# Queries and keys of a dilated attention placed by SBUF transfers, softmax statistics of two heads exchanged by a matmul

## The chip, the cores and the metric

One core of one Trainium2 chip runs the whole program in one launch. The metric is the device time in microseconds; a figure for a kernel is the median of its runs.

## What is computed

Two blocks on a sequence of 1024 positions and 1024 channels, in f32: an S5 mixer with a conv-GLU FFN, then a dilated attention with a second FFN. The change lies in the attention. It has 16 heads of 64 channels and three dilation groups g = 0, 1, 2 (dilation 1, 4, 16), each with queries, keys and values of its own; every group is an attention over a band of 128 steps, and the groups are merged by their log-sum-exps:

```python
for g, (_, dil) in enumerate(DILATED_GROUPS):       # dil = 1, 4, 16
    s = jnp.einsum('brnqhe,brnkhe->brnhqk', qb, kb) + bias
    s = jnp.where(valid[:, None], s, NEG_BIG)
    lse = jax.nn.logsumexp(s, axis=-1)
    p = jnp.exp(s - lse[..., None])
    o = jnp.einsum('brnhqk,brnkhe->brnqhe', p, vb)
...
wts = jax.nn.softmax(jnp.stack(lses), axis=0)
o = jnp.einsum('gblh,gblhe->blhe', wts, jnp.stack(outs))
```

## The kernel before

Every large matmul keeps f32 accuracy by splitting each operand into a high part (`wh`, a cast to fp32r) and the rest (`wl`), and issuing three matmuls, `mm3` on L88, L89 and L90. A weight of 512 KB is loaded to `raw`, cast to `wh` by ScalarE (ACT, L83), and `wl` is subtracted by VectorE (DVE, L84). The order of the instructions of every engine is fixed when the program is built: a scheduler places them by its own timeline. On the chip each engine, and the DMA queue of SyncE (SP) too, runs its list in order and waits at an instruction until its inputs and its buffer are there.

The attention (L367) runs over 8 pairs of heads; a pair fills the 128 partitions, head 0 on the lower 64 rows and head 1 on the upper 64. For each pair and each g, `proj` (L407) makes Q and K in two halves of 512 columns, 24 matmuls (`qk` in the traces) to a half, then `scores` (L463) multiplies them (`s`, L488), and DVE adds the bias and takes the row maxima (L476). `proj` of the next pair's g = 0 is issued ahead of `output` (L583) of this one, and the scheduler interleaves further. `output` takes the exponentials (`exps`, L526), the softmax factors of each head (`softmax`, L539), scales the probabilities `p1` (g = 0, L556) and `p4` (g = 1 and 2, L563), transposes them on TensorE (PE, `t`, L604) and multiplies them by V (`o`, L614), and adds the two parts to `oT` (L658), which goes to DRAM as `oscr`.

A score also is two matmuls: `qs` holds the query's high part of one head on 64 rows and its low part on the other 64, and `qs` and `kl` of K hold the key's high and low part on both halves of the rows. So each 64-row half has to reach the other half of the partitions. Before, ACT copies the PSUM result to `tmp` (named `qt`, L430, L432) and casts the 64-row halves (L436, L438), and GpSimd (POOL) subtracts the low parts (L440), with different partitions in and out.

The g = 0 rows and the g = 1, 2 rows of a query lie on different partitions, so the two softmax statistics (maximum and sum) have to be exchanged: 32 small copies of 32 partitions on DVE per head and direction pair (L551, L552), followed by `factor` (L565), once for f1 and once for f4.

The pools matter: `w` has 6 tiles, that is three split weights, in the whole program after the S5 part; `raw` has 2; PSUM has two tiles for `qk` (psA) and four for `s` and `t`, which share them (psS).

## Time and profile before

| | |
|---|---|
| median of 3 runs | 3187.31 us (3179.75 to 3188.91) |
| the profiled execution | 3185.67 us |
| its span, first to last instruction | 3183.7 us, so 1.97 us lie outside |
| busy in the span: PE, DVE, ACT, POOL | 2963.2, 1809.4, 1074.7, 721.9 us |
| mean granted clock of TensorE | 0.961 of full speed |
| the attention | from about 1410 us to 2333 us |

PE is busy for 93% of the span; where it stands still, or runs at half its clock, time is lost. The attention repeats with a period of one pair, which can be cut at the start of the first `p1` scaling of each pair (1500.31, 1612.86, ... 2175.86 us). The tail from 2175.86 us on holds the output of pair 6, the last scores and the output of pair 7, which has no further `proj` beside it.

### The profile page before, as it was taken

The page shows a single profiled execution, that of the slowest core. Times are in us where ns is not written, and L with a number is a line of the kernel's source. Part 1 is how long each engine was busy: PE and PEld are TensorE (multiplying, and loading weights), DVE is VectorE, ACT ScalarE, POOL GpSimd, SP SyncE. Part 2 cuts the span into 40 slices and gives each one's busy share as a digit, 9 for nine tenths or more (in the row PEclk, how much of TensorE's full clock was granted, in tenths as well). Part 3 has the DMA queues.
Part 4 walks back from the last instruction along what each step waited for, and adds up shares of the span by engine and source line. Part 5 has one row for each costly group of instructions (what it writes and reads, how often), then busy time and mean ns, then how long its engine had stood idle before and what let it go on. Part 6 is the DMA issues. An engine that isn't in the chain of part 4 may idle for free.

```text
span 3183.7 us, 36883 instructions
## 1 busy us (share of the span) xinstructions
PE 2963.2 (93%) x14422; PEld 2457.5 (77%) x14422; DVE 1809.4 (57%) x3348; ACT 1074.7 (34%) x1868; POOL 721.9 (23%) x543
## 2 busy tenths in 40 slices
PE   4789999999999999999898998989689999999997
PEld 3668878888888879998677777767567788888886
DVE  8964774544545541115668567666757644445446
ACT  2433332222222231126455555645523322222222
POOL 7920050000000000015335434434652300000001
PEclk8889999999999999999999999999799999999998
DMA  5232421111111232321111111111243211111111
GB/s 174 58 126 62 135 71 47 47 49 51 52 48 40 81 122 88 92 86 41 57 50 57 55 62 44 57 60 44 70 150 112 66 47 53 47 53 41 53 60 53
DMA packets 98413, 219.63 MB, mean 69 GB/s; under 512 B 9664, under 2 KB 51248, under 8 KB 98240
## 3 DMA queue, kind: packets, MB, share of 16 engines
q1 hardware_dynamic: 96128, 207.85, 20.8%
q0 software_dynamic: 2112, 9.44, 0.9%
q8 instruction: 113, 1.85, 0.2%
q14 instruction: 60, 0.49, 0.0%
HBM read 191.49 MB, written 35.20 MB: 71 GB/s over the span
## 4 chain that ended last, share of the span: by engine, by line
PE 78%; DVE 11%; POOL 5%; ACT 3%; DMA 1%; issue 1%; SPq 0%; ACTq 0%; POOLq 0%; DVEq 0%
PE dn L236 15%; PE up L89 10%; PE up L88 10%; PE up L90 10%; PE qk L88 3%; PE qk L89 3%; PE qk L90 3%; PE v L88 3%; DVE p L556 3%; PE v L89 3%; PE v L90 3%; PE o L614 3%; ACT p L533 2%; PE t L604 2%; PE s L488 2%; DVE p L563 2%
## 5 line engine op out<-in xcount | busy, mean ns | idle before, releaser
L84 DVE TENSOR_TENSOR wl<-raw,wh 128x1024 fp32r<-128x1024 f32 x261 | 339.3, 1301 | 680.4 <-ACT wh L83 675.8
L83 ACT CAST wh<-raw 128x1024 fp32r<-128x1024 f32 x261 | 274.0, 1052 | 1081.2 <-PE up L89 468.6
L88 PE MATMUL up<-hT,wh 128*128 128x512 f32 x1408 | 548.7, 391 | 12.1 <-DVE u L212 12.1
L89 PE MATMUL up<-hT,wh 128*128 128x512 f32 x1408 | 548.9, 390 | 0.7 <-DVE hT L84 0.7
L90 PE MATMUL up<-hT,wl 128*128 128x512 f32 x1408 | 548.5, 390 | 0.0
L440 POOL TENSOR_TENSOR qs<-qt,qs 64x512 fp32r<-64x512 f32 x96 | 127.4, 1327 | 1174.7 <-ACT qs L436 1140.9
L88 PEld LDWEIGHTS up<-hT,wh 128*128 128x128 f32 x1408 | 265.0, 188 | 67.5 <-issue 12.9
L440 POOL TENSOR_TENSOR kl<-qt,qs 64x512 fp32r<-64x512 f32 x192 | 255.8, 1332 | 253.9 <-PE s L488 218.8
L88 PE MATMUL qk<-hT,wh 128*128 128x512 f32 x768 | 310.6, 404 | 0.0
L89 PEld LDWEIGHTS up<-hT,wh 128*128 128x128 f32 x1408 | 265.4, 188 | 56.9 <-DVE hT L84 2.1
L90 PEld LDWEIGHTS up<-hT,wl 128*128 128x128 f32 x1408 | 265.1, 188 | 54.9
L90 PE MATMUL qk<-hT,wl 128*128 128x512 f32 x768 | 306.8, 399 | 0.0
L89 PE MATMUL qk<-hT,wh 128*128 128x512 f32 x768 | 306.4, 399 | 0.0
L212 DVE SCALAR_TENSOR_TENSOR u<-up,cw,u 128x1022 f32<-128x1022 f32 (+1 forms) x176 | 224.6, 1278 | 30.4 <-ACT u L208 28.2
L246 DVE TENSOR_TENSOR acc<-acc,dn 128x1024 f32<-128x1024 f32 x144 | 175.0, 1217 | 91.8 <-PE dn L236 89.3
L236 PE MATMUL dn<-wh,ah 128*128 128x512 f32 x704 | 216.9, 389 | 0.0
L236 PE MATMUL dn<-wl,ah 128*128 128x512 f32 x704 | 216.7, 389 | 0.0
L236 PE MATMUL dn<-wh,al 128*128 128x512 f32 x704 | 216.6, 389 | 0.0
L88 PEld LDWEIGHTS qk<-hT,wh 128*128 128x128 f32 x768 | 148.8, 194 | 30.2 <-issue 2.7
L89 PEld LDWEIGHTS qk<-hT,wh 128*128 128x128 f32 x768 | 148.1, 193 | 29.1
L90 PEld LDWEIGHTS qk<-hT,wl 128*128 128x128 f32 x768 | 147.4, 192 | 29.5
L604 PE MATMUL t<-ident,p 128*128 128x128 f32 x624 | 105.3, 316 | 64.7 <-DVE p L556 64.7
(248 smaller groups left out, 5113.9 us busy)
## 6 DMA issues: line engine op xcount, KB each, us to landing
raw<-in_w_up SPq DMA_DIRECT2D x88, 512.0 KB, 3.5
raw<-in_w_out SPq DMA_DIRECT2D x48, 512.0 KB, 3.5
raw<-in_w_down SPq DMA_DIRECT2D x44, 512.0 KB, 3.5
raw<-in_w_v SPq DMA_DIRECT2D x25, 512.0 KB, 3.6
vscr<-vs SPq DMA_DIRECT2D x48, 256.0 KB, 2.3
V<-vscr SPq DMA_DIRECT2D x24, 512.0 KB, 4.1
raw<-in_w_q SPq DMA_DIRECT2D x24, 512.0 KB, 3.6
raw<-in_w_k SPq DMA_DIRECT2D x24, 512.0 KB, 3.5
```

Source lines behind the costliest of these rows:

```text
L83: nc.scalar.copy(hi, x)
L84: (eng or nc.vector).tensor_tensor(out=lo, in0=x, in1=hi.bitcast(F32), op=ALU.subtract)
L88: nc.tensor.matmul(out, lh, rh, start=first, stop=False)
L89: nc.tensor.matmul(out, lh, rl, start=False, stop=False)
L90: nc.tensor.matmul(out, ll, rh, start=False, stop=last)
L212: nc.vector.scalar_tensor_tensor(out=tf[:, d:], in0=ps[:, : T - d], scalar=cw[:, d, ft : ft + 1], in1=tf[:, d:], op0=ALU.mult, op1=ALU.add,)
L236: nc.tensor.matmul(ps[:, h * 512 : h * 512 + 512], l_, w[wi][:, h * 512 : h * 512 + 512], start=(i == 0 and l_ is ah and wi == 0), stop=(i ...
L246: nc.vector.tensor_tensor(out=accs[tt][:], in0=accs[tt][:], in1=ps[:], op=ALU.add)
L440: nc.gpsimd.tensor_tensor(out=lo, in0=tmp[r], in1=hi.bitcast(F32), op=ALU.subtract)
L556: nc.vector.tensor_scalar(out=x, in0=x, scalar1=f1[:, n : n + 1], scalar2=None, op0=ALU.mult)
L604: nc.tensor.transpose(ps[:, i * P : i * P + P], b, net.ident[:])
L614: nc.tensor.matmul(o[64 * h : 64 * h + 64, oc], v[:, 64 * h : 64 * h + 64], pt[h], start=st, stop=sp_)
```

## The change

`proj` no longer uses GpSimd. ACT writes the high part `qh` (128x512) straight from PSUM (now the key carries the factor 0.125), DVE subtracts the low part `ql` (128x512) from PSUM, and SBUF-to-SBUF DMAs on SP's queue put the 64-row halves in place: 4 for a half of Q, 8 for a half of K, so 24 to a g, 72 to a pair and 576 in all, 64 rows of 2 KB each.

`softmax` treats both heads together. `exchange` multiplies the statistics by a mask (`bd`, DVE), and one matmul with a constant matrix `eye4` moves them to the partitions where they are wanted; four small copies read them from PSUM. There is one such matmul for the statistics, one factor chain of half the instructions, and one matmul that brings the factor back for `p4`. Head 1's `p4` is scaled by ACT, head 0's by DVE.

For room, the pool `w` goes from 6 tiles to 4 (two split weights, in the whole program after the S5 part), `values_first` keeps two weights of the first values block and not three (one more load of 512 KB in the attention), `q` goes from 9 to 10 tiles and `qt` from 2 to 4.

```diff
-    ws = [net.wload(net.a["w_v"][0, i], **({"pool": pool, "tag": "x"} if i == 3 else {})) for i in range(4)]
+    ws = [net.wload(net.a["w_v"][0, i], **({"pool": pool, "tag": "x"} if i > 1 else {})) for i in range(4)]
...
-        tmp = ap.tile([P, 512], F32, "qt", "qt")
...
+        hi, lo = (ap.tile([P, 512], F32R, "qt", n) for n in ("qh", "ql"))
...
+        if isq:
+            nc.scalar.copy(h_, i)
+            nc.vector.tensor_tensor(out=l_, in0=i, in1=h_.bitcast(F32), op=ALU.subtract)
         else:
-            nc.scalar.copy(o, i)
+            nc.scalar.mul(h_, i, 0.125)
+            nc.vector.scalar_tensor_tensor(
+                out=l_, in0=i, scalar=0.125, in1=h_.bitcast(F32), op0=ALU.mult, op1=ALU.subtract
+            )
         for h in range(2):
-            r, o = slice(64 * h, 64 * h + 64), slice(64 - 64 * h, 128 - 64 * h)
-            hi = X[h][r, sl]
-            nc.scalar.copy(hi, tmp[r])
-            if not isq:
-                nc.scalar.copy(X[h][o, sl], tmp[r])
-            for lo in [X[h][o, sl]] if isq else [kl[h][r, sl], kl[h][o, sl]]:
-                nc.gpsimd.tensor_tensor(out=lo, in0=tmp[r], in1=hi.bitcast(F32), op=ALU.subtract)
+            r = slice(64 * h, 64 * h + 64)
+            for c in range(2):
+                o = slice(64 * c, 64 * c + 64)
+                if isq:
+                    nc.sync.dma_start(X[h][o, sl].bitcast(F32), (lo if c else hi)[r].bitcast(F32))
+                else:
+                    nc.sync.dma_start(X[h][o, sl].bitcast(F32), hi[r].bitcast(F32))
+                    nc.sync.dma_start(kl[h][o, sl].bitcast(F32), lo[r].bitcast(F32))
...
+    def exchange(self, st, n, a, b):
+        bd = net.asp.tile([P, 4, 32], F32, "bd", "bd")
+        nc.vector.tensor_tensor(
+            out=bd[:, :, : 8 * n], in0=st.unsqueeze(1).broadcast_to([P, 4, 8 * n]),
+            in1=net.mask4[:].unsqueeze(2).broadcast_to([P, 4, 8 * n]), op=ALU.mult,
+        )
+        ps = net.psS.tile([P, 512], F32, "s", "x")
+        nc.tensor.matmul(
+            ps[:, : 32 * n], net.eye4[:], bd[:, :, : 8 * n], start=True, stop=True
+        )
...
+        for c in range(8):
+            for h in range(2):
+                p = self.tiles4(h)[c][1]
+                if h:
+                    nc.scalar.mul(p, p, f4[:, h, c : c + 1])
+                else:
+                    nc.vector.tensor_scalar(out=p, in0=p, scalar1=f4[:, h, c : c + 1], scalar2=None, op0=ALU.mult)
...
-        net.weight_pools(6, 2)
+        net.weight_pools(4, 2)
```

The scheduler orders everything anew. Three places of its lists follow; numbers after a name are those of its tiles, and `waits` names the engines or DMA lanes whose semaphores an instruction waits for.

First place, DVE between the exponentials of a pair and its first transposes. Before, from the last scaling of head 0's `p4` (L563) on:

```order
L563 TENSOR_SCALAR p4_1262_9222<-p4_1262_9222,e_1361_9935 128x512
L84 TENSOR_TENSOR wl_1463_10536<-raw_1461_10533,wh_1462_10535 128x1024 [waits DMAHW7_49,PE_49,Activation_49]
L576 TENSOR_TENSOR t_1370_10016<-st1_1264_9224,e_1368_10010 128x8 [waits Activation_49]
L569 TENSOR_TENSOR M_1371_10022<-st4_1265_9225,x4_1366_9975 128x8
L577 TENSOR_TENSOR ex_1369_10011<-x1_1365_9974,ex_1369_10011 128x8 [waits Activation_49]
L571 TENSOR_TENSOR e_1372_10024<-st4_1265_9225,M_1371_10022 128x8 [waits DVE_49]
L572 TENSOR_TENSOR ex_1373_10025<-x4_1366_9975,M_1371_10022 128x8
L578 TENSOR_TENSOR t_1370_10016<-t_1370_10016,ex_1369_10011 128x8 [waits DVE_49]
L579 RECIPROCAL t_1370_10016<-t_1370_10016 128x8 [waits DVE_49]
L576 TENSOR_TENSOR t_1374_10030<-st4_1265_9225,e_1372_10024 128x8 [waits Activation_49]
L577 TENSOR_TENSOR ex_1373_10025<-x4_1366_9975,ex_1373_10025 128x8 [waits Activation_49]
L580 TENSOR_TENSOR e_1368_10010<-e_1368_10010,t_1370_10016 128x8 [waits DVE_49]
```

Behind these rows stands the scaling of head 1's `p1`. Now, from the end of the one factor chain on:

```order
L584 TENSOR_TENSOR g4_1383_9962<-e_1380_9951,M_1379_9950 128x16 [waits DVE_49]
L587 TENSOR_TENSOR f1_1386_9968<-e_1380_9951,M_1379_9950 128x16
L550 TENSOR_TENSOR bd_1384_9964<-g4_1383_9962,mask4_1089_7705 128x4x16 [waits DVE_49]
L596 TENSOR_SCALAR p1_1269_9241<-p1_1269_9241,f1_1386_9968 128x128 [waits DVE_49]
L596 TENSOR_SCALAR p1_1269_9241<-p1_1269_9241,f1_1386_9968 128x256 x7
L596 TENSOR_SCALAR p1_1270_9242<-p1_1270_9242,f1_1386_9968 128x128
L596 TENSOR_SCALAR p1_1270_9242<-p1_1270_9242,f1_1386_9968 128x256 x7
L84 TENSOR_TENSOR wl_1479_10498<-raw_1477_10495,wh_1478_10497 128x1024 [waits PE_49,Activation_49]
L433 TENSOR_TENSOR ql_1457_10350<-qk_1455_10324,qh_1456_10349 128x512 [waits DMAHW4_49,DMAHW2_49,DMAHW6_49,DMAHW0_49,Activation_49]
L590 COPY f4_1382_9961<-x_1385_9966 32x16 [waits PE_49]
L590 COPY f4_1382_9961<-x_1385_9966 32x16 x3
```

The `p1` of both heads is now scaled in a row (L596, 16 instructions), ahead of all `p4`, which follows behind the four copies from the second exchange.

Second place, the change from one pair to the next: the last `s` of g = 0 or g = 1 of the next pair. PE before, from the last `s` of g = 0 on:

```order
L488 MATMUL s_1433_10312<-kl_1345_9797,qs_1334_9725 128x256
L90 MATMUL qk_1468_10572<-hT_1079_7656,wl_1463_10536 128x512
L88 MATMUL qk_1468_10572<-hT_1082_7666,wh_1462_10535 128x512
L89 MATMUL qk_1468_10572<-hT_1082_7666,wh_1462_10535 128x512
L90 MATMUL qk_1468_10572<-hT_1082_7666,wl_1463_10536 128x512
L88 MATMUL qk_1468_10572<-hT_1084_7675,wh_1462_10535 128x512
L89 MATMUL qk_1468_10572<-hT_1084_7675,wh_1462_10535 128x512
L90 MATMUL qk_1468_10572<-hT_1084_7675,wl_1463_10536 128x512
L88 MATMUL qk_1468_10572<-hT_1087_7685,wh_1462_10535 128x512
L89 MATMUL qk_1468_10572<-hT_1087_7685,wh_1462_10535 128x512
L90 MATMUL qk_1468_10572<-hT_1087_7685,wl_1463_10536 128x512
L488 MATMUL s_1455_10479<-qs_1447_10405,qs_1438_10335 128x128 [waits DVE_49,Pool_49]
```

PE now, from the end of the last but one `s` tile of g = 1 on:

```order
L495 MATMUL s_1475_10481<-qs_1462_10364,qs_1451_10290 128x256
L495 MATMUL s_1475_10481<-kl_1464_10366,qs_1451_10290 128x256
L495 MATMUL s_1476_10488<-qs_1462_10364,qs_1451_10290 128x256 [waits DVE_49]
L495 MATMUL s_1476_10488<-kl_1464_10366,qs_1451_10290 128x256
L495 MATMUL s_1476_10488<-qs_1462_10364,qs_1451_10290 128x256
L495 MATMUL s_1476_10488<-kl_1464_10366,qs_1451_10290 128x256
L88 MATMUL qk_1495_10579<-hT_1029_7405,wh_1489_10571 128x512 [waits DVE_49]
L89 MATMUL qk_1495_10579<-hT_1029_7405,wh_1489_10571 128x512
```

Before, ten `qk` stand between the `s` of g = 0 and those of g = 1. Now three `qk` stand in the middle of g = 0 and none between g = 0 and the end of g = 1; the next `qk` tile waits for DVE. DVE now, at the same place:

```order
L483 ISA mg_1436_10206 128x1
L483 ISA p4_1433_10203,mg_1436_10206<-s_1476_10488,bt_1346_9748 128x256 [waits PE_49]
L483 ISA mg_1436_10206 128x1
L483 ISA p4_1433_10203,mg_1436_10206<-s_1476_10488,bt_1346_9748 128x256
L483 ISA mg_1436_10206 128x1
L433 TENSOR_TENSOR ql_1484_10529<-qk_1482_10503,qh_1483_10528 128x512 [waits DMAHW5_49,DMAHW3_49,DMAHW6_49,DMAHW1_49,Activation_49]
L433 TENSOR_TENSOR ql_1487_10562<-qk_1485_10536,qh_1486_10561 128x512 [waits DMAHW5_49,DMAHW7_49,DMAHW2_49,Activation_49]
L436 SCALAR_TENSOR_TENSOR ql_1497_10605<-qk_1495_10579,qh_1496_10604 128x512 [waits DMAHW4_49,DMAHW3_49,Activation_49]
L84 TENSOR_TENSOR wl_1521_10791<-raw_1519_10788,wh_1520_10790 128x1024 [waits PE_49,Activation_49]
L436 SCALAR_TENSOR_TENSOR ql_1500_10642<-qk_1498_10616,qh_1499_10641 128x512 [waits DMAHW7_49,DMAHW0_49,Activation_49]
```

The low part `ql` that frees the `qk` tile (L433) stands behind all maxima (L483, ISA, with the reading of its accumulator) of g = 0 and g = 1.

Third place, SP's queue at the same change of pairs. Before, from the loads of V for the next output on:

```order
L588 DMA V_1508_10894<-vscr_7476 128x1024 [waits DMAHW3_49,PE_49]
L588 DMA V_1509_10896<-vscr_7476 128x1024 [waits DMAHW4_49,DMAHW1_49,PE_49]
L665 DMA oscr_9062<-oT_1392_10125 128x1024 [waits DMAHW5_49,DVE_49]
L75 DMA raw_1602_11425<-in_w_k 128x1024 [waits DMAHW0_49,DVE_49]
L75 DMA raw_1619_11559<-in_w_q 128x1024 [waits DMAHW2_49,DVE_49]
L453 DMA bt_1487_10737<-bscr0_2300 32x2x256 [waits DVE_49]
L453 DMA bt_1487_10737<-bscr0_2300 32x2x256 x2
```

Now:

```order
L610 DMA V_1532_10872<-vscr_7476 128x1024 [waits DMAHW5_49,PE_49]
L610 DMA V_1533_10874<-vscr_7476 128x1024 [waits DMAHW6_49,DMAHW1_49,PE_49]
L683 DMA oscr_9075<-oT_1404_10079 128x1024 [waits DMAHW7_49,DVE_49]
L446 DMA qs_1462_10364<-qh_1466_10392 64x512 [waits DMAHW0_49,PE_49]
L447 DMA kl_1464_10366<-ql_1467_10393 64x512 [waits PE_49]
L446 DMA qs_1462_10364<-qh_1466_10392 64x512 [waits DMAHW2_49]
L447 DMA kl_1464_10366<-ql_1467_10393 64x512 [waits DMAHW3_49]
L446 DMA qs_1462_10364<-qh_1469_10429 64x512 [waits DMAHW4_49]
L447 DMA kl_1464_10366<-ql_1470_10430 64x512 [waits DMAHW5_49]
L446 DMA qs_1462_10364<-qh_1469_10429 64x512 [waits DMAHW6_49]
L447 DMA kl_1464_10366<-ql_1470_10430 64x512 [waits DMAHW7_49]
```

Behind the two loads of V and the store of `oT` stand eight placements of K, g = 1, head 1; most of them also wait for an earlier DMA on the same lane (DMAHW).

## Rows read from the trace of the kernel before

**Rows 1.** The page, busy us (share of the span) and instructions of each engine.

```profile
PE 2963.2 (93%) x14422; PEld 2457.5 (77%) x14422; DVE 1809.4 (57%) x3348; ACT 1074.7 (34%) x1868; POOL 721.9 (23%) x543
```

**Rows 2.** Stretches (us): each engine busy and (instructions), clock, DMA share, GB/s.

```profile
1500.31:1612.86 112.55, 103.67 (x567) 82.85 (x566) 77.33 (x248) 60.73 (x138) 47.95 (x36) 0.95 0.18 55
...
2175.86:2290.00 114.14, 88.08 (x477) 69.18 (x475) 72.45 (x228) 57.89 (x134) 56.92 (x44) 0.87 0.16 56
```

**Rows 3.** Timeline of PE around the longest gap of a period: start us, us, instruction.

```profile
1632.80 1.97 PE L604 MATMUL t<-ident,p 128*128 128x128 f32 x8 [5.50 <-DVE p L556]
...
1638.34 0.63 PE L89 MATMUL qk<-hT,wh 128*128 128x512 f32 x1
1638.77 0.63 PE L90 MATMUL qk<-hT,wl 128*128 128x512 f32 x1
...
1642.05 0.40 PE L89 MATMUL qk<-hT,wh 128*128 128x512 f32 x1
1642.28 0.40 PE L90 MATMUL qk<-hT,wl 128*128 128x512 f32 x1
```

**Rows 4.** Timeline of DVE, scaling of the probabilities.

```profile
1612.66 8.62 DVE L556 TENSOR_SCALAR p<-p,e 128x128 f32<-128x128 f32 x8
...
1623.40 6.91 DVE L563 TENSOR_SCALAR p<-p,e 128x256 f32<-128x256 f32 x8
...
1636.84 2.73 DVE L563 TENSOR_SCALAR p<-p,e 128x256 f32<-128x256 f32 x8
...
2296.97 2.13 DVE L556 TENSOR_SCALAR p<-p,e 128x128 f32<-128x128 f32 x8
```

**Rows 5.** Groups by line and form, 1400 to 2300 us: count | busy us, mean ns.

```profile
L440 POOL TENSOR_TENSOR kl<-qt,qs 64x512 fp32r<-64x512 f32 x192 | 255.8, 1332 | 253.9 <-PE s L488 218.8 <-ACT qs L436 21.6 <-issue 2.2
...
L84 DVE TENSOR_TENSOR wl<-raw,wh 128x1024 fp32r<-128x1024 f32 x46 | 58.9, 1280 | 48.4 <-ACT wh L83 48.4
...
L533 ACT ACTIVATE p<-p,nm 128x512 f32<-128x512 f32 x64 | 45.5, 711 | 0.0
...
L579 DVE RECIPROCAL t<-t 128x8 f32<-128x8 f32 x30 | 6.0, 201 | 0.8
```

**Rows 6.** Timeline of DVE behind the last output of a pair.

```profile
1673.87 1.22 DVE L658 TENSOR_TENSOR oT<-oT,o 128x1024 f32<-128x1024 f32 x1 [5.50 <-PE o L614]
1675.01 0.28 DVE L476 CUSTOM_DVE_ANT_0 p<-s,bt 128x128 f32<-128x128 f32 x1
...
1675.22 0.42 DVE L476 CUSTOM_DVE_ANT_0 p<-s,bt 128x256 f32<-128x256 f32 x1
...
1675.56 0.42 DVE L476 CUSTOM_DVE_ANT_0 p<-s,bt 128x256 f32<-128x256 f32 x1
```

**Rows 7.** What PE waited for, 1400 to 2300 us: us, times, longest us.

```profile
PE s L488 <- DVE st L476: 16.4, 14, 1.5
```

**Rows 8.** Timeline of the SP queue: start us, us of issue, transfer, count.

```profile
1673.65 0.80 SPq L588 DMA_DIRECT2D V<-vscr  x2
1675.12 0.32 SPq L665 DMA_DIRECT2D oscr<-oT  x1
...
1716.43 1.74 SPq L453 DMA_DIRECT2D bt<-bscr  x4
```

**Rows 9.** DMA issues of the whole span: count, KB each, median us to landing.

```profile
oscr<-oT SPq DMA_DIRECT2D x7, 512.0 KB, 5.7
...
bt<-bscr SPq DMA_DIRECT2D x32, 64.0 KB, 1.9
```

**Rows 10.** The 20 us in which the DMA engines moved most, columns as in rows 2.

```profile
2340.00:2360.00 20.00, 17.17 (x72) 13.56 (x71) 5.20 (x4) 3.15 (x3) 14.67 (x6) 0.97 0.76 287
```

**Rows 11.** Timeline of POOL in the last pair.

```profile
2274.84 5.27 POOL L440 TENSOR_TENSOR kl<-qt,qs 64x512 fp32r<-64x512 f32 x4
...
2300.22 11.02 POOL L563 TENSOR_SCALAR p<-p,e 128x256 f32<-128x256 f32 x8 [3.31 <-DVE e L571]
```

**Rows 12.** What PE waited for, 225 to 460 us.

```profile
PE up L88 <- DVE u L212: 6.0, 1, 6.0
```

More of the change, by code (lines that the diff above doesn't have):

```diff
@@ L373, in attention @@
         else:
-            ws = ws + [net.wload(net.a["w_v"][0, 3], pool=ap, tag="q")]
+            ws = ws + [net.wload(net.a["w_v"][0, i], pool=ap, tag="q") for i in (2, 3)]
         for j in range(8) if blk else range(4, 8):
@@ L463, in scores @@
     def scores(self, g):
-        net, nc, ap, sp, bt = self.net, self.net.nc, self.ap, self.net.small, self.bt
+        net, nc, ap, sp, bt = self.net, self.net.nc, self.ap, self.net.asp, self.bt
         if g == 0:
@@ new lines, in softmax @@
+    def softmax(self):
+        nc, sp = self.net.nc, self.net.asp
+        t = lambda shape, n: sp.tile([P] + shape, F32, n, n)
+        st1, st4 = self.st1, self.st4
+        x = t([2, 2, 8], "x1")
+        ps = self.exchange(st4[:].rearrange("p h s c -> p (h s c)"), 4, "r", "n")
+        for r in range(4):
+            R = slice(32 * r, 32 * r + 32)
+            nc.vector.tensor_copy(
+                x[R].rearrange("p h s (n a) -> p (h s) a n", a=4), ps[R, :, :, r, :]
+            )
+        M, e, y = t([2, 8], "M"), t([2, 2, 8], "e"), t([2, 2, 8], "y")
+        nc.vector.tensor_tensor(out=M[:], in0=st1[:, :, 0], in1=x[:, :, 0], op=ALU.max)
+        for i, s in enumerate((st1, x)):
+            nc.vector.tensor_tensor(out=e[:, i], in0=s[:, :, 0], in1=M[:], op=ALU.subtract)
+        nc.scalar.activation(e[:], e[:], AF.Exp)
+        for i, s in enumerate((st1, x)):
+            nc.vector.tensor_tensor(out=y[:, i], in0=s[:, :, 1], in1=e[:, i], op=ALU.mult)
+        nc.vector.tensor_tensor(out=M[:], in0=y[:, 0], in1=y[:, 1], op=ALU.add)
+        nc.vector.reciprocal(M[:], M[:])
+        f4 = t([2, 8], "f4")
+        g = t([2, 8], "g4")
+        nc.vector.tensor_tensor(out=g[:], in0=e[:, 1], in1=M[:], op=ALU.mult)
+        ps = self.exchange(g[:].rearrange("p h c -> p (h c)"), 2, "n", "a")
+        f1 = t([2, 8], "f1")
+        nc.vector.tensor_tensor(out=f1[:], in0=e[:, 0], in1=M[:], op=ALU.mult)
+        for a in range(4):
+            A = slice(32 * a, 32 * a + 32)
+            nc.vector.tensor_copy(
+                f4[A].rearrange("p h (r n) -> p h r n", r=4), ps[A, :, :, :, a]
+            )
+        for h in range(2):
+            for n in range(8):
+                p = self.p1[h][:, n, 128 if n == 0 else 0 :]
+                nc.vector.tensor_scalar(out=p, in0=p, scalar1=f1[:, h, n : n + 1], scalar2=None, op0=ALU.mult)
+        for c in range(8):
+            for h in range(2):
+                p = self.tiles4(h)[c][1]
[3 more added lines that the diff above has]
+                    nc.vector.tensor_scalar(out=p, in0=p, scalar1=f4[:, h, c : c + 1], scalar2=None, op0=ALU.mult)
@@ L589, in output @@
             V.append(v)
-        for h in range(2):
-            if self.hp < 7:
+        if self.hp < 7:
+            for h in range(2):
                 self.exps(h)
-            f4 = self.softmax(h)
-            if self.hp == 7 and h == 0:
-                self.scale4(h, f4, nc.gpsimd)
-        if self.hp == 7:
-            self.scale4(1, f4, nc.vector)
+        self.softmax()
         def transposed(blocks):
@@ L673, in setup @@
     net.psO = net.pool("psO", ctx, PSUM, o=1)
-    return net.pool("ap", ctx, q=9, qt=2, V=2, oT=1, p1=2, p4=2, bt=1, pt=4)
+    net.asp = net.pool("asp", ctx, eye4=1, mask4=1, bd=1, x1=1, y=1, g4=1, other=2)
+    net.eye4 = net.asp.tile([P, P], F32, "eye4")
+    net.mask4 = net.asp.tile([P, 4], F32, "mask4")
+    net.nc.sync.dma_start(net.eye4[:], net.a["eye4"])
+    net.nc.sync.dma_start(net.mask4[:], net.a["mask4"])
+    return net.pool("ap", ctx, q=10, qt=4, V=2, oT=1, p1=2, p4=2, bt=1, pt=4)
 MAGIC = 12582912.0
@@ L1416, in layout @@
     o["eye16"] = np.tile(np.eye(16, dtype=np.float32), (8, 1))
+    o["eye4"] = np.tile(np.eye(32, dtype=np.float32), (4, 4))
+    o["mask4"] = np.repeat(np.eye(4, dtype=np.float32), 32, axis=0)
     o["onehot"] = bias_onehot()
```

61 lines of the change are left out of this document (11 added, 50 removed).

## The prediction

> **What bounds the kernel now.** First the page: PE is busy for 93% of the span, DVE for 57%, POOL for 23% [rows 1]. Less work on DVE, ACT or POOL is thus worth nothing by itself; time can come only out of PE's gaps, or out of stretches in which PE runs at half its clock. Then the stretches by pair: a period is 112.6 us, with 103.4 busy on PE, so 9.2 us idle, and a granted clock of 0.95 [rows 2]. Six such periods lie between 1500.31 and 2175.86 us, 112.59 on average. The longest gap is in the timeline of PE: 5.50 us until DVE has scaled `p1` of head 1, and when PE comes back, its matmuls run at the lower of the two clock levels: two neighbouring `qk` start 0.43 us apart, some microseconds later 0.23 [rows 3]. 16 `t` (8 in 1.97 us, taken as twice their full-clock time) and 9 `qk` (0.20 each) pay about 4 us; I use 4.2. A pair therefore is 103.4 - 4.2 = 99.2 us of work at full clock, 4.2 of low clock and 9.2 of idling.
>
> Why `p1` of head 1 is late stands in the order of DVE and in its timeline. Its scaling comes behind head 0's `p1` scaling (8.62 us), head 0's `p4` scaling (6.91) and the chain of factors. The same eight instructions took 2.13 us at 2297 us, and `p4` took 2.73, when POOL ran no L440 beside them [rows 4]. POOL makes four such subtractions of 1.33 us for each half of K [rows 5].
>
> **The change, part by part.** The sum is made against the profiled execution, 3185.67 us, which stands 1.6 us below the median of the runs. About 0.3% of the median, 9.6 us, is what a measurement of this kernel can tell from no change.
>
> *Gaps before the transposes.* Both heads' `p1` are now scaled one behind the other, ahead of `p4`. By the rows without POOL this is 2 x 2.13 = 4.3 us. Behind the last `s` of the pair PE has 64 `qk` ahead of the first exchange, 14.6 us at 0.23; head 1's eight exponentials, two `qh` and a weight cast on ACT are under 12 x 0.75 = 9, an exponential of 512 columns being 0.71 [rows 5]: some 5 us to spare. Between the exchanges lie 37 `qk`, 8.4 us; four copies, the chain and `bd`, 16 small instructions of 0.2 [rows 5], and one `ql` are 3.9, 4.5 to spare. Then come the scalings, 4.3, of which the first two suffice for the first `t`. The 5.50 us gap, its smaller neighbours (about 1.5 us) and the 4.2 us of low clock go. What is late next is the `pt` copy on DVE behind head 0's `p4` scaling: 2.73 + four small copies against some 4 us of `qk` and `t`; I put 1.0 us there. The two exchange matmuls cost 0.4 at most, two `t` at the low clock being 0.5 [rows 3]. ACT's new scaling of head 1's `p4`, eight passes of at most 0.71 us [rows 5], is hidden by the `o` of g = 0.
>
> *Projections.* ACT goes from five passes per half of K, and three of Q, to one each; it was hidden and stays so. DVE gains 12 `ql` a pair: a pass over 512 columns of PSUM is bounded by two passes of 256 with the bias added, 0.35 us each, thus 0.7 [rows 6], and from below by 0.35; I take 0.7. POOL's 36 L440 a pair go. Where `ql` waits for nobody it is hidden; at the change of pairs it is not.
>
> *The change of pairs.* Let T0 be the end of the last `o`, 1673.8 us in the rows. DVE then does the `oT` addition (1.14 us to the next start), two heads of g = 0 with one row of 128 and seven of 256 columns (0.21 + 7 x 0.345 = 2.63 each), one `wl` (1.2, its mean is 1.28 with POOL beside it [rows 5]), two negations (0.4), two heads of g = 1 (4 x 0.21 + 4 x 0.345 = 2.2 each) and only then `ql`: 1.14 + 5.26 + 1.2 + 0.4 + 4.4 + 0.7 = 13.1 us [rows 6]. PE has 29 `s` of g = 0, three `qk` and 32 `s` of g = 1, about 7.6 us at 0.12 and 0.23 us. So 5.5 us of idling, in pieces at each `s` tile that waits for DVE; the longest, before the `qk`, is what DVE still owes then: six rows of 256, four of 128 and `ql` less one `s` tile, some 3.3 us. Before, ten `qk` lay there and PE waited 16.4 us in 14 pieces, none over 1.5 [rows 7], 2.3 a pair; those are replaced, not added.
>
> *The placements.* Half a K is eight issues; an issue is 0.43 us, by the four `bt` DMAs in 1.74 [rows 8], and lands in 1.9 us (64 KB over 32 partitions [rows 9]). From PSUM on that is 0.7 (ACT) + 0.7 (`ql`) + 8 x 0.43 + 1.9 = 6.7 us. For K of g = 2 PE has 24 `qk` of the next half, or 32 `qk` with some `s`, in between, 5.5 + 3.2 and 8 us: hidden. Past SP's queue it is less clear at the change of pairs: eight placements of K, g = 1, head 1, stand behind two V loads (issued at T0) and the `oscr` store, which waits for `oT` (T0 + 1.3) [rows 8]. The store itself landed 5.7 us after its issue [rows 9], T0 + 7. The first placements, four issues later, may land at T0 + 7.5 to 8.5, the last at T0 + 9 to 10; the `s` of head 1 want them at about T0 + 7.9 and T0 + 9. I put 0.7 us a pair there; the bounds are 0 and 5.3 (below).
>
> *A period* is then 99.2 + 0.4 + 1.0 + 5.5 + 0.7, and 0.8 for small waits that a walk does not see (half of the smaller gaps of now): 107.6 us, 5.0 less. Six periods: **-30**.
>
> *The tail* from 2175.86 us has pair 6's output, like a period (-5), and the last pair, where nothing covers the chain. There POOL's last K parts end at 2280.1 [rows 11], while by the placements' chain they would be there some 6 us earlier, of which the maxima on DVE keep 1 to 2: -4. The first `p1` scaling starts only at 2296.97 us [rows 4], behind the last copies and two factor chains; with 16 small instructions of 0.2 less on that path and two exchanges more I put -2 (0 to -5). POOL's 11.02 us for head 0's `p4` [rows 11] become 2.73 on DVE [rows 4] beside at most 8 x 0.71 on ACT: -6. In all **-17**, between -8 and -25.
>
> *The `w` ring.* With two weights and not three, a weight can be cast only when the last but one is used up. A cast and `wl` are about 2.4 us (`wl` 1.28 [rows 5], the cast no longer than that), hidden by the 11 us of a weight with 48 matmuls, but hardly by one with 12 (2.7 us) in the two output projections, nor at the start of each FFN, where PE waits 6.0 us now [rows 12] after three interleaved tiles; now two are interleaved, and the third comes in the gap. I put +3 for each of two layers, **+6**, from -4 to +14. The one more load of `w_v` I put at **+1**: it can cost nothing, or at most its share of the 20 us at 287 GB/s [rows 10], 1.8 us.
>
> Sum: -30 - 17 + 6 + 1 = -40, so 3145.67, **3145 us**.
>
> **The rivals.** *The clock falls at every change of pairs.* 5.5 us of idling lowered it, waits of at most 1.5 did not [rows 3, 7]; the 3.3 us piece lies between. It would cost the 4.2 us again, seven times: +29, **3174 us**. Against it speaks that the idle time comes in pieces.
>
> *The change of pairs costs no more than now.* If the chip drains the maxima faster than my walk, 2.3 us stay of 6.2 [rows 7]: 7 x 3.9 = 27 less, **3118 us**.
>
> *Placements at half the transfer rate, behind V and `oscr`: slower than before.* The 16 DMA engines moved 287 GB/s in their fullest 20 us [rows 10]. If a transfer of 64 partitions gets half of that, 128 KB take 0.91 us. At the change of pairs 1.5 MB (V, V, `oscr`) go first, 5.5 us at 287 GB/s, then eight placements, 7.3 us, and 1.5 to the semaphore (the 1.9 us [rows 9] less the transfer): the last is there at T0 + 14.3 and wanted at T0 + 9. PE then waits 5.3 us in one piece, the clock falls as it did after 5.50, and a change costs 5.3 + 4.2 - 0.7 = 8.8 more; seven are 62: **3207 us**. It turns the sign when a change of pairs loses over 5.7 us more than I say (40 / 7). For it: SP's queue is in order. Against it: 32 partitions landed in 1.9 us [rows 9], and elsewhere even 0.91 us each just fits the cover. The Trainium skill ("SBUF — State Buffer", section "Door 1: The DMA port swizzle") says that 64 neighbouring partitions reach only 8 of 16 ports, and gives 196 GB/s for them; by it a placement would be 0.67 us, an estimate, the last lands at T0 + 12.4, 3.4 late, and with 7 x (3.4 - 0.7) the time would be 3164 us. No row here has a transfer of 64 partitions.
>
> *The ring of two decides*, or the change does not do what it says: 6 us more at each FFN start and 1 us at each of 16 weights of the two output projections, 2 x (6 + 16) = 44: **3189 us**.
>
> **How the numbers follow.** The forecast has a chance of 0.50, with 3120 to 3170 as its own range; the falling clock 0.17, the cheap change of pairs 0.10, the slow placements 0.15, the ring 0.08. The bound for faster is 3177.7 us. Faster: 0.48 + 0.10 + 0.10 + 0.02 + 0.02 = 0.72; within: 0.02 + 0.06 + 0.01 + 0.04 = 0.13; slower: 0.01 + 0.12 + 0.02 = 0.15. The range, 3105 to 3200 us, leaves out about 0.08 above (the worse half of the slow placements) and as much below (a period of 99.5 us without any idling).
>
> **What would show it.** Right: periods of 106 to 109 us, no wait of `t` for the scaling of `p1` over 1 us, waits of `s` and `qk` for DVE of 5 to 6 us a pair at its start, DVE busy under 60 us a pair, no POOL work; a clock near 1.00 in the pairs. Wrong: a clock below 0.97 there (first rival); PE or its weight loads waiting for DMA into `qs` or `kl` by microseconds (third); `up` or `wo` waiting longer for `wh` or `wl` (fourth). A period above 112.6 us would refute the whole walk.

## The result and the profile after

The changed kernel takes **3147.92 us** (median of 4 runs, 3147.12 to 3154.18), the kernel before, on the same chip, 3186.01 (3179.75 to 3188.91): ratio 0.9887, 95% interval 0.9868 to 0.9907, so 36 us less by the ratio. Forecast were 3145 us, range 3105 to 3200. The profiled execution took 3147.12 us.

The page of the kernel after, engines over the whole span of 3145.1 us, against [rows 1]:

```profile
PE 2964.7 (94%) x14454; PEld 2456.0 (78%) x14454; DVE 1598.8 (51%) x2773; ACT 922.7 (29%) x1589; POOL 329.7 (10%) x247
```

DVE, ACT and POOL have lost 211, 152 and 392 us of work, the span 38.6. PE has as much as before [rows 1]: what has gone is idle time of PE. The stretches between the first `p1` scalings of neighbouring pairs, against [rows 2]:

```profile
1509.52:1617.40 107.88, 104.42 (x568) 83.63 (x567) 48.37 (x176) 41.72 (x102) 0.00 (x0) 0.95 0.56 145
1617.40:1725.89 108.49, 104.33 (x568) 83.40 (x567) 48.36 (x175) 41.73 (x102) 0.00 (x0) 0.95 0.55 143
1725.89:1832.85 106.96, 103.17 (x568) 82.45 (x567) 48.28 (x175) 41.72 (x102) 0.00 (x0) 0.97 0.56 146
```

A period is 107.97 us on average over six, (2157.32 - 1509.52) / 6, where 112.59 was and 107.6 was forecast. PE's idle time fell from 9 us to about 4, but the clock stayed at 0.95 to 0.97. POOL does nothing here any more, and the DMA engines are busy for 0.56 instead of 0.18.

What PE waited for, 1400 to 2300 us, of the kernel after (us in total, times, longest):

```profile
PE x L555 <- DVE bd L550: 15.6, 2, 9.7
PE s L495 <- DMA qs<-qh: 13.6, 12, 2.7
PE qk L88 <- DVE ql L433: 10.4, 7, 1.5
PE s L495 <- DVE st L483: 4.3, 6, 0.7
PE o L632 <- DVE pt L625: 2.5, 1, 2.5
```

The same list of the kernel before has at its head

```profile
PE t L604 <- DVE p L556: 63.8, 28, 15.5
```

This wait of `t` for the scaling of `p1` is gone. The waits of `x` (the exchange matmul) lie in the last pair, where nothing covers the chain. The three below it make up the change of pairs. One of these on PE's timeline (start, us, instruction, idle time and its releaser); the last `o` of the pair before ends at about 1663.6 us, T0:

```profile
1669.95 0.39 PE L495 MATMUL s<-qs,qs 128*128 128x256 f32 x1 [0.72 <-DVE st L483]
...
1672.71 0.30 PE L495 MATMUL s<-qs,qs 128*128 128x128 f32 x1 [1.26 <-DMA qs<-qh]
...
1674.82 0.55 PE L495 MATMUL s<-qs,qs 128*128 128x256 f32 x1 [0.55 <-DMA qs<-qh]
...
1676.35 0.41 PE L495 MATMUL s<-qs,qs 128*128 128x256 f32 x1
1676.57 0.41 PE L495 MATMUL s<-kl,qs 128*128 128x256 f32 x1
1678.45 0.79 PE L88 MATMUL qk<-hT,wh 128*128 128x512 f32 x1 [1.47 <-DVE ql L433]
...
1683.31 0.63 PE L90 MATMUL qk<-hT,wl 128*128 128x512 f32 x1
...
1685.03 0.40 PE L90 MATMUL qk<-hT,wl 128*128 128x512 f32 x1
```

Four waits of 1.5 us at most, 4.0 together. The clock falls behind the first two of them, 0.72 and 1.26 us, and is low already when PE waits for `ql`. From there on matmuls run at half speed: `s` 0.22 us apart instead of 0.12, twelve `qk` 0.43 apart instead of 0.23. The stretches of the kernel after around it say the same, with the clock ahead of the last two figures:

```profile
1669.20:1673.70 4.50, 2.36 (x15) 1.85 (x15) 4.44 (x31) 3.69 (x15) 0.00 (x0) 1.00 1.06 250
1673.90:1683.90 10.00, 7.98 (x23) 6.33 (x23) 3.78 (x18) 4.82 (x19) 0.00 (x0) 0.50 0.57 149
1684.00:1690.00 6.00, 6.00 (x27) 4.95 (x27) 0.69 (x1) 0.60 (x1) 0.00 (x0) 1.00 0.17 38
```

By these distances low clock costs 8 x 0.1 + 12 x 0.2 = 3.2 us at this change of pairs; half of the 7.98 us for which PE is busy at 0.50 makes 4.0. The clock falls at all seven changes of pairs, each time ahead of the wait for `ql`.

By stages of the whole kernel, each from a first matmul to the next stage's first (us; differences are taken before rounding):

| stage | before | after | difference |
|---|---|---|---|
| S5, up to its output projection `z` | 209.1 | 205.0 | -4.1 |
| `z` to the first `wo` | 90.0 | 88.8 | -1.2 |
| first `wo` to `up` | 90.2 | 95.3 | +5.2 |
| first `up` to `dn` | 100.5 | 98.3 | -2.2 |
| first `dn` to the values | 633.4 | 633.2 | -0.2 |
| values, `v` to the first `qk` | 281.2 | 282.1 | +0.8 |
| attention, `qk` to the second `wo` | 929.3 | 887.5 | -41.8 |
| second `wo` to `up` | 98.8 | 106.1 | +7.3 |
| second `up` to `dn` | 101.3 | 98.8 | -2.5 |

The first two lines, -5.3, are not counted as a gain of the change: up to `z` PE's instructions stand in the same order in both kernels, and in the runs below `z` begins between 202.9 and 209.8 us, and lasts 87.2 to 90.0, with no relation to the edit. The profiled execution of the kernel after is also the fastest of its four.

### The profile page after: what moved, and what is told of

The parts are those of the page before. It is cut to its first block, busy times and chain, and to the rows that moved or that the text cites. A ratio compares the mean times of both kernels' runs of the same rounds, so it can differ in the third digit from the quotient of the medians.

```text
span 3145.1 us, 36960 instructions
## 1 busy us (share of the span) xinstructions
PE 2964.7 (94%) x14454; PEld 2456.0 (78%) x14454; DVE 1598.8 (51%) x2773; ACT 922.7 (29%) x1589; POOL 329.7 (10%) x247
## 5 line engine op out<-in xcount | busy, mean ns | idle before, releaser
L84 POOL TENSOR_TENSOR gT<-oraw,gT 128x512 fp32r<-128x512 f32 x14 | 18.0, 1302 | 1796.2 <-ACT gT L83 1791.8
L88 PEld LDWEIGHTS qk<-hT,wh 128*128 128x128 f32 x768 | 148.3, 193 | 41.8 <-DVE ql L433 12.4
L88 PE MATMUL v<-wh,hT 128*128 128x512 f32 x384 | 152.8, 400 | 1.0 <-DVE tmp L174 1.0
L236 PEld LDWEIGHTS dn<-wl,ah 128*128 128x128 f32 x704 | 132.1, 188 | 27.5
```

The costliest lines, as they stand in the source:

```text
L84: (eng or nc.vector).tensor_tensor(out=lo, in0=x, in1=hi.bitcast(F32), op=ALU.subtract)
L88: nc.tensor.matmul(out, lh, rh, start=first, stop=False)
L236: nc.tensor.matmul(ps[:, h * 512 : h * 512 + 512], l_, w[wi][:, h * 512 : h * 512 + 512], start=(i == 0 and l_ is ah and wi == 0), stop=(i ...
```

## The experiments

The question was which of the two parts brings the gain, and what the rest of the change of pairs and the smaller `w` ring cost. "Before" is the kernel before on the same chip.

| run | median us | before | ratio, 95% interval | period us | attention us |
|---|---|---|---|---|---|
| before | 3186.01 | | | 112.6 | 929.3 |
| the change | 3147.92 | 3186.01 | 0.9868 to 0.9907 | 108.0 | 887.5 |
| softmax only | 3138.80 | 3179.83 | 0.9855 to 0.9892 | 106.6 | 886.2 |
| placements only | 3165.44 | 3179.83 | 0.9941 to 0.9967 | 109.0 | 901.9 |
| third weight outside the attention | 3150.94 | 3179.83 | 0.9890 to 0.9924 | 108.1 | 890.8 |
| third weight in the projections | 3147.79 | 3181.29 | 0.9862 to 0.9917 | 108.4 | 895.3 |
| V and `oscr` on POOL's queue | 3164.43 | 3179.83 | 0.9938 to 0.9970 | 110.7 | 903.7 |
| order written otherwise | 3183.43 | 3181.29 | 0.9986 to 1.0015 | 112.6 | 929.2 |
| order forced | 3173.62 | 3180.96 | 0.9963 to 0.9983 | 111.1 | 919.1 |
| hybrid | 3133.10 | 3181.29 | 0.9815 to 0.9867 | 105.5 | 878.6 |
| hybrid, ring | 3132.60 | 3181.29 | 0.9810 to 0.9865 | 105.6 | 876.9 |
| `ql` first | 3137.19 | 3180.96 | 0.9845 to 0.9878 | 105.0 | 872.9 |
| `ql` first, third weight outside | 3133.27 | 3184.75 | 0.9829 to 0.9867 | 105.7 | 876.8 |
| `ql` first, third weight in projections | 3127.77 | 3184.75 | 0.9812 to 0.9842 | 105.6 | 876.5 |

**Softmax only.** The changed kernel with `proj`, `values_first` and the pools of the kernel before:

```diff
-            nc.vector.tensor_tensor(out=l_, in0=i, in1=h_.bitcast(F32), op=ALU.subtract)
...
+                nc.gpsimd.tensor_tensor(out=lo, in0=tmp[r], in1=hi.bitcast(F32), op=ALU.subtract)
...
-        net.weight_pools(4, 2)
+        net.weight_pools(6, 2)
```

> The new softmax of both heads alone: Q and K are made as before (ACT casts, GpSimd low parts, no placements), w ring of three as before. Theory A (the gain comes from GpSimd's end: its subtractions stretch DVE's scaling): with GpSimd still there the 16 scalings of p1 in a row take about 17 us beside it, PE still waits microseconds for them with the clock falling behind it, periods stay at 110 to 114 us, total 3170 to 3195. Theory B (the gain comes from the new softmax: fewer DVE instructions and p1 of both heads ahead of p4): the gap before the transposes goes without the placements' costs, periods of 103 to 106 us, total 3120 to 3145.

Measured: 3138.80 us, in theory B's range, and an attention of 886.2, as short as with the whole change. DVE's timeline and PE's waits of this run (L589 is the scaling of `p1`):

```profile
1615.45 8.37 DVE L589 TENSOR_SCALAR p<-p,f 128x128 f32<-128x128 f32 x16
```

```profile
PE t L615 <- DVE p L589: 21.0, 23, 1.0
PE s L488 <- POOL kl L440: 8.9, 3, 4.2
```

The same row on DVE's timeline of the kernel after:

```profile
1617.40 4.15 DVE L596 TENSOR_SCALAR p<-p,f 128x128 f32<-128x128 f32 x16
```

With POOL beside it the scaling still takes twice as long, though not the 17 us of theory A. But it now stands ahead of `p4`, so `t` waits in pieces of at most 1.0 us, some three to a pair, and the clock holds:

```profile
1615.45:1721.77 106.32, 102.30 (x566) 81.15 (x566) 52.76 (x163) 63.69 (x138) 48.89 (x36) 0.98 0.18 58
```

At 0.98 this is the highest clock of a period so far. The new softmax alone is enough.

**Placements only.** The changed kernel with the softmax of the kernel before, head by head:

```diff
-        self.softmax()
+            f4 = self.softmax(h)
+            if self.hp == 7 and h == 0:
+                self.scale4(h, f4, nc.gpsimd)
```

> The placements alone: qh, ql and the SBUF transfers and the pools of the changed kernel, but the softmax of before, one head after the other with its 32-row copies on DVE. Theory A (GpSimd's end): scaling of p1 and p4 without GpSimd beside it is 2.1 and 2.7 us, so p1 of head 1 is ready some 9 us earlier and the 5.5 us gap shrinks to under 1; periods of 107 to 110 us, total 3145 to 3160. Theory B (the new softmax): p1 of head 1 still comes behind p4 of head 0 and two more chains; PE still waits over 3 us before the transposes, and the losses at the change of pairs come on top: periods of 112 to 116 us, total 3180 to 3210.

Measured: 3165.44 us, between the ranges of the two theories, attention 27 us shorter than before. DVE's groups by form of this run (L563 is here the scaling of `p1`), and two of PE's waits:

```profile
L563 DVE TENSOR_SCALAR p<-p,e 128x256 f32<-128x256 f32 x112 | 33.2, 358 | 0.0
```

```profile
PE qk L88 <- DVE ql L433: 22.0, 9, 3.1
PE t L611 <- DVE p L563: 17.9, 3, 16.3
```

The group of before to set beside it:

```profile
L556 DVE TENSOR_SCALAR p<-p,e 128x256 f32<-128x256 f32 x105 | 89.2, 914 | 0.0
```

Without POOL's subtractions the same scaling takes 358 ns instead of 914; `p1` of head 1 is there in time although its place in the order is the old one, and the wait for it is gone but for the last pair (16.3). That is theory A, and so is the period; the total is 5 us above its range, with that wait left in the last pair and waits of `qk` for `ql` of up to 3.1 us. So each part closes the 5.50 us gap [rows 3] by itself. The gains in the attention, 43 and 27 us, don't add: together they are 42. In the steady pairs the placements bring nothing on top of the softmax; the period is 1.4 us longer with them and their pools. No run separates the placements there from the smaller `w` pool in the attention.

**Third weight outside the attention; in the projections only.** Every third weight goes to a pool of its own, two tiles, which is there in the dense layers; the second version leaves it out in the FFNs:

```diff
+        if pool is None:
+            self.wi += 1
+            pool = self.wx if self.wx and self.wi % 3 == 0 else self.wp
...
+                net.wx = net.pool(f"wx{l}", c, w=2)
```

> The changed kernel with a third split weight again in the two S5 projections, output projections and FFNs (two more w tiles that live only outside the attention). Theory: the output projections' extra 12 us (wo to up: 95.3 and 106.2 us now, 90.2 and 98.8 before) are the ring of two; they go back to 90 and 99 us, while the FFN starts take back the 2.3 us each that the less interleaved order had won: total 3136 to 3142. Rival: the output projections wait for weights from DRAM or for the layer norm, whatever the ring: total within 3 us of the changed kernel's 3148.

> The changed kernel with the third split weight in the two S5 projections and output projections alone, not in the FFNs. Theory (the ring of two costs in the output projections and gains at the FFN starts): output projections of 90 and 97 us, FFN starts (up to dn) of 98 to 100 us, so 10 to 12 us less than the changed kernel outside the attention, total 3132 to 3140. Rival (the gain at the FFN starts hangs on the projections' order and goes with it): as in the run with the ring of three everywhere, 102 us, total 3140 to 3150.

Measured: 3150.94 and 3147.79 us, no gain: the totals of the two rivals. The projections did as expected: they are back at 90.2 and 97 us (95.3 and 106.1 with the change), 14 us less. But the FFN starts take 102.6 and 101.9 us in the first run and 100.9 and 101.0 in the second (98.3 and 98.8 with the change), so 7.4 and 4.8 us go again; in the second, 98 to 100 were expected, so part of the gain there hung on the projections, as its rival says. The values are 2.9 and 2.4 us longer. And the attention is 3.3 and 7.8 us longer, though its own code and pools are the same, 2.5 and 5.1 of it behind the first `p1` scaling of pair 6, in the tail. The scheduler made other lists; which row of them costs the time was not found.

**V and `oscr` on POOL's queue**, so that nothing stands ahead of the placements on SP's:

```diff
-            nc.sync.dma_start(v[:], net.vscr[g, self.hp])
+            nc.gpsimd.dma_start(v[:], net.vscr[g, self.hp])
...
-            nc.sync.dma_start(net.oscr[self.hp], oT[:])
+            nc.gpsimd.dma_start(net.oscr[self.hp], oT[:])
```

> The changed kernel with the loads of V and the store of oT issued on GpSimd's queue, which is idle in the attention; the placements are no longer behind them in SP's list, though they share the DMA engines. Theory (the placements at the change of pairs are late because SP's list is in order and 1.5 MB go first): PE's waits for placed tiles, 13.6 us in 12 pieces now, go under 4 us, a change of pairs is 1 to 2 us shorter: total 3134 to 3142. Rival (DVE's row of maxima sets the end of the change of pairs): those waits go, but PE waits as long for DVE: total 3145 to 3150.

Measured: 3164.43 us; by the ratios that is some 21 us more than the change (0.9954 against 0.9887). SP's queue at a change of pairs of this run, T0 = 1669.6 us, and PE's waits:

```profile
1669.06 0.33 SPq L75 DMA_DIRECT2D raw<-in_w_q  x1
1670.98 0.46 SPq L446 DMA_DIRECT2D qs<-qh  x1
...
1673.27 2.38 SPq L447 DMA_DIRECT2D kl<-ql  x1
```

```profile
PE s L495 <- DMA qs<-qh: 32.8, 8, 5.4
```

The placements issue from T0 + 1.4, a little earlier than with the change (T0 + 1.7), but one issue lasts 2.38 us, and a weight of 512 KB, which the scheduler moved up, goes ahead of them. Neither theory had this. V, `oscr` and the weight were still moved beside the placements; another queue took no bytes away: `oscr` landed in 8.0 us (5.9 with the change), V in 5.5 (4.4). The Trainium skill ("Trainium Kernel Development and Optimization", section "Key Constraints") says that the queues of SP, ACT and POOL run on the same 16 DMA engines, and that a second one saves only time of issue; this run agrees.

**Order written otherwise; order forced.** The kernel before, with both heads' `p4` scaled only after both softmaxes. In the first version that is the order in the source alone; in the second head 0's factor takes in 0 times a column of head 1's `p1`, so that it can't be ready earlier:

```diff
-            self.scale4(h, f4, nc.vector)
...
+            nc.vector.scalar_tensor_tensor(
+                out=f[:], in0=self.p1[1][:, 7, 248:256], scalar=0.0, in1=f4[0][:], op0=ALU.mult, op1=ALU.add
+            )
+            self.scale4(0, f, nc.vector)
```

> The kernel before with one edit: the scaling of p4 of both heads comes behind the softmax and p1 scaling of both. No exchange matmul, no placements, ring of three. Theory (the gap before the transposes is DVE's order, p1 of head 1 behind p4 of head 0): PE's 5.5 us wait goes, periods of 103 to 107 us, total 3140 to 3155 on a chip where the kernel before takes 3180. Rival (the number of small copies and the two chains keep DVE late, only the exchange removes them): the gap shrinks by the 6.9 us of p4 at most in part, p4 turns late instead, periods of 110 to 113 us, total 3165 to 3185.

> The kernel before with the order of the run before forced: head 0's p4 scaling takes its factor through a small instruction that also reads head 1's scaled p1, so it cannot come ahead of it (in the run before the scheduler had left DVE's list as it was). No exchange matmul, no placements. Theory (the gap before the transposes is DVE's order): p1 of head 1 is ready some 7 us earlier, PE's 5.5 us wait and the low clock behind it go, periods of 103 to 107 us, total 3135 to 3155 where the kernel before takes 3181. Rival (the two chains and the small copies are what the exchange saves; order alone moves the wait to p4): p4 of both heads beside GpSimd is late for its transposes instead, periods of 109 to 113 us, total 3165 to 3185.

Measured: 3183.43 us for the first; the scheduler put DVE's list back as it was, gap and all (5.49 us), so it says nothing on the order. The forced version took 3173.62 us, and its PE timeline has

```profile
1733.86 0.74 PE L608 MATMUL t<-ident,p 128*128 128x128 f32 x2 [4.30 <-DVE p L556]
```

With the order forced, the wait is 1.2 us shorter than the 5.50 [rows 3], and the attention 10 us. The total is in the rival's range, but the wait did not move to `p4`, as the rival says: it still is for `p1` of head 1. The first `t` comes 17.1 us behind the start of head 0's `p1` scaling, 3.0 sooner than before (20.1), but the scheduler also put 1.8 us less of PE's work ahead of it. Between the two `p1` scalings DVE still needs 7.1 us, with two `wl` and the chain of factors, whose small instructions become long beside POOL's subtractions. Two of the same line on DVE's timeline of this run, the second with POOL at L440 beside it:

```profile
1726.41 0.15 DVE L574 TENSOR_TENSOR t<-st,e 128x8 f32<-128x8 f32 x1
1728.52 1.25 DVE L574 TENSOR_TENSOR t<-st,e 128x8 f32<-128x8 f32 x1
```

The rest of the new softmax's 43 is then left to what else it changes: the factor chains and copies of the two heads that became one chain and a matmul, and head 1's `p4` on ACT. These were not taken apart.

**Hybrid.** Softmax only, with placements in the last pair alone; then with a third weight outside the FFNs only:

```diff
-            proj(net, net.wload(net.a[w][hp, g]), self.hT, g, w == "w_q", self.ap) for w in ("w_q", "w_k")
+            (proj_dma if hp == 7 else proj)(net, net.wload(net.a[w][hp, g]), self.hT, g, w == "w_q", self.ap) for w in ("w_q", "w_k")
```

> The new softmax with GpSimd's Q and K of before in pairs 0 to 6, and the placements in the last pair alone; ring of three. Theory (the placements pay only where no next pair covers the chain): periods as in the run with the new softmax alone (818 us from the first to the last qk there), and the end from the last qk to the output projection as in the changed kernel (59 us, against 68 in that run): total 8 to 10 us under that run, 3126 to 3133. Rival (the end is the exponentials and the chain, whatever makes K): within 3 us of it.

> The hybrid (new softmax, GpSimd's Q and K in pairs 0 to 6, placements in the last pair), and in the FFNs a ring of two split weights, of three elsewhere. Theory: the hybrid less 2 to 3 us at each FFN start: 3121 to 3128. Rival as in the run before: no change against the hybrid.

Measured: 3133.10 and 3132.60 us. From the last `qk` to the output projection it is 63.5 us, against 68.1 with softmax only and 59.0 with the change: in the last pair, where POOL's parts are on the path (`s` waits for `kl` there, 8.9 us in the rows of softmax only), the placements do pay, though less than expected: `s` there waits 6.3 us for a placement instead. The attention is 7.6 us shorter than with softmax only. By the starts of the `p1` scalings 6.1 of them lie in the last of the six periods, 100.6 us instead of 106.7; the first five are as long as there, so the 105.5 of the table is no gain of a steady pair. The ring of two in the FFNs takes 1.2 and 0.7 us off their starts, not 2 to 3, and makes no difference in the total.

**`ql` first.** The changed kernel, with `qh` and `ql` ahead of the maxima in the scheduler's order:

```diff
+        with net.tc.high_priority():
-        if isq:
+            if isq:
```

> The changed kernel with qh and ql at the highest priority of the scheduler; at the change of pairs ql of Q moves 21 rows up in DVE's list, ahead of the last maxima of g = 1, and its qh ahead of seven of the eight exponentials of head 0 on ACT. Theory (DVE's row of maxima ahead of ql sets the end of a change of pairs): the 1.5 us wait of qk for ql goes, 1 to 2 us less a pair, total 3134 to 3143 where the changed kernel takes 3145. Rival (ql cannot start earlier, since qh's tile is freed by the placements of K, which land late): DVE waits for qh in the middle of the maxima, the same or longer: total 3143 to 3155.

Measured: 3137.19 us, attention 14.6 us shorter than with the change. DVE's timeline and PE's at a change of pairs of this run, T0 again about 1663.6:

```profile
1673.21 0.69 DVE L434 TENSOR_TENSOR ql<-qk,qh 128x512 fp32r<-128x512 f32 x1 [0.30 <-DMA qs<-qh]
```

```profile
1676.79 0.41 PE L496 MATMUL s<-kl,qs 128*128 128x256 f32 x1
1677.01 0.63 PE L88 MATMUL qk<-hT,wh 128*128 128x512 f32 x1
...
1679.14 0.63 PE L90 MATMUL qk<-hT,wl 128*128 128x512 f32 x1
...
1680.11 0.40 PE L90 MATMUL qk<-hT,wl 128*128 128x512 f32 x1
```

`ql` runs at T0 + 9.6 and no longer at T0 + 14.1. The `qk` follow the last `s` without a gap, 1.47 us less, and six of them run at the low clock and not twelve, 1.2 less. That is 2.7 of the 3.0 us by which the period fell. The clock still falls here, behind waits of 0.71 and 1.07 us; so it falls without the wait for `ql` too. Six periods give 18 us; 3.4 are lost again in the tail.

**The two together.** `ql` first, with the third weight as in the two runs above:

> The changed kernel with qh and ql first in the scheduler and the third split weight outside the attention. Theory (the two gains lie in different stages and add): attention 873 us as with ql first, output projections of 90 and 97 us, FFN starts of 102: total 6 to 8 us under the run with ql first, 3128 to 3133. Rival (what the third weight wins is lost in the order of values and attention, as in the run with it alone): 3135 to 3142.

> As the run before, with the third split weight only in the projections, not in the FFNs. Theory (the gains add): attention 873 us, output projections of 90 and 97 us, FFN starts of 98 to 101: total 3125 to 3132. Rival (the order of values and attention changes with it and loses as much): 3135 to 3142.

Measured: 3133.27 and **3127.77 us**. The second beats both kernels: 57 us under the kernel before beside it, and by the ratios some 19 under the change (0.9827 against 0.9887). Here the third weight in the projections kept about half of its gain: 90.2 and 96.3 us in them, 14.5 less than with `ql` first alone, but 4.0 lost at the FFN starts and 3.5 in the attention. The rest of the difference between the two profiled executions lies ahead of `z`, and is not counted.

## Why the prediction was right, and where it was not

**The size** was right: 3147.9 us against 3145, a period of 107.97 against 107.6. So was the sign, and the main terms have theirs: the attention gave 41.8 us, 27.7 in the six periods where -30 stood and 14.1 around them where -17 stood; the ring cost 12.5 in the projections and gave 4.7 back at the FFN starts, +7.8 where +6 stood. The values took 0.8 more where +1 stood for the load of `w_v`, but they took as long with softmax only (282.0), which has no such load. These terms make -33 us, against 40 forecast and 36 by the ratio; the rest of the two profiled executions' difference lies ahead of `wo` and is not counted.

**The gap before the transposes** went as forecast: both heads' `p1` take 4.15 us (4.3 forecast), no `t` waits for them, and its low clock is gone. What failed in this step is the cause behind it. It was told of the change as a whole; the runs show that either half of the change closes the gap, so that the second half had nothing left to gain in these pairs. The 1.0 us that was put on `pt` isn't there: one wait of 2.5 in the whole attention.

**The change of pairs** is the step that failed, behind a right total. Forecast were 6.2 us of idling there, 1.8 of other small waits in the period and no low clock, 8.0 in all, on 99.6 us of work. Measured are 108.49 - 104.33 = 4.2 us of idling in the period of the rows above, 3.2 to 4.0 of low clock, and so 100.3 to 101.1 of work at full clock. The idling was overstated, the clock was taken as safe and the work was put some 1 us too low. That these errors cancel is luck.

The idling was overstated because PE's own work at the change was put at 7.6 us. 61 `s` at 0.12 and three `qk` at 0.23 are 8.0 already; and of the 14.9 us from T0 to the `qk` behind `ql`, PE worked 10.9, about 1 of it for the low clock. Where the other 1 us of work in a period comes from was not found.

The first rival's mechanism, a clock that falls at every change of pairs, came true, at about its price (3.2 to 4.0 of 4.2 us); its condition, one piece of 3.3 us, did not. The argument against it, that the idle time comes in pieces, is what failed: the clock fell behind two waits of 0.72 and 1.26 us, 2.0 together. Of the prediction's own signs, the waits for DVE of 5 to 6 us a pair (0.72 + 1.47 here) and a clock near 1.00 are missing, and the clock below 0.97 stands in its list for wrong. Before, waits of that size had left the clock up [rows 7], not only single ones. PE's timeline and the stretch of the kernel before at the change of pairs show 1.53 and 0.80 us, 2.3 together, and a clock of 1.00:

```profile
1687.46 0.39 PE L488 MATMUL s<-qs,qs 128*128 128x256 f32 x1 [1.53 <-DVE st L476]
...
1690.16 0.33 PE L488 MATMUL s<-qs,qs 128*128 128x128 f32 x1 [0.80 <-DVE st L476]
```

```profile
1685.90:1692.00 6.10, 3.77 (x22) 3.05 (x22) 5.88 (x28) 1.74 (x6) 3.06 (x3) 1.00 0.00 0
```

So the sum of the waits does not decide it either. What makes the difference was not tried.

`ql` was forecast to take 0.7 us (0.69) and to start 12.4 us behind T0. It starts at T0 + 14.1, because the maxima ahead of it wait themselves, 0.67 and 0.92 us, for `s` of head 1, which waits for its placements and then runs at half clock. DVE's timeline of the kernel after:

```profile
1674.31 0.29 DVE L483 CUSTOM_DVE_ANT_0 p<-s,bt 128x128 f32<-128x128 f32 x1 [0.67 <-PE s L495]
...
1676.17 0.42 DVE L483 CUSTOM_DVE_ANT_0 p<-s,bt 128x256 f32<-128x256 f32 x1 [0.92 <-PE s L495]
...
1677.71 0.69 DVE L433 TENSOR_TENSOR ql<-qk,qh 128x512 fp32r<-128x512 f32 x1
```

**The placements** were late by more than forecast. SP's queue of the kernel after, and the landings in its list of DMA issues (count, KB each, median us):

```profile
1665.33 0.47 SPq L446 DMA_DIRECT2D qs<-qh  x1
1665.85 1.06 SPq L447 DMA_DIRECT2D kl<-ql  x1
1666.97 1.21 SPq L446 DMA_DIRECT2D qs<-qh  x1
...
1670.95 0.60 SPq L447 DMA_DIRECT2D kl<-ql  x1
```

```profile
qs<-qh SPq DMA_DIRECT2D x288, 128.0 KB, 2.4
kl<-ql SPq DMA_DIRECT2D x192, 128.0 KB, 2.4
...
oscr<-oT SPq DMA_DIRECT2D x7, 512.0 KB, 5.9
```

An issue takes 0.60 us, up to 1.21 behind V and `oscr`, not the 0.43 taken from the `bt` DMAs [rows 8]; a landing 2.4, not 1.9 [rows 9]. The last `qs` of head 1 comes at T0 + 11.2, where T0 + 9 to 10 was forecast: 1.26 + 0.55 us of waiting, not 0.7. While PE waits for them, the DMA engines have no room left: the stretch 1669.20:1673.70 above has them busy throughout (1.06, 250 GB/s). The third rival with T0 + 14.3 overstated it. The Trainium skill's "SBUF — State Buffer" ("Door 1: The DMA port swizzle"), from whose 196 GB/s the prediction worked out, as an estimate, 0.67 us to a transfer of 64 partitions and T0 + 12.4, came nearer than that rival, but the wait of 3.4 us in one piece isn't there. The run on POOL's queue shows that a greater lateness costs in kind what the rival said: waits of `s` of up to 5.4 us, and 21 us in all.

**The ring** had the right size, not the right place: all of its cost lies in the two output projections (in the second, PE's waits for `wh` and `wl` grew from 3.9 to 9.5 us), while the FFN starts, where 6.0 us of waiting stood [rows 12], became 2.2 and 2.5 us shorter. In the fourth rival's sum the 16 weights of the two projections are counted twice: as it is worded, 2 x 6 + 16 = 28 us more, 3173 us and not 3189.

**The tail** was forecast at -17; the start of the first pair had no term. By the starts of the `p1` scalings (in the kernel before they lie 0.2 us ahead of the cuts, 1612.66 [rows 4] for 1612.86) the tail behind pair 6's is -25.3, 158.1 to 132.8 us, and the stretch ahead of the first is +11.2, since `p1` of both heads now starts later in its pair. Only the two together, -14, can be set beside -17.
